# A down projection in two column chunks at once, with seven block products in place of eight for 14 of its 44 pair steps

## The chip, the cores and the metric

The kernel runs on one core of one Trainium2 chip. The metric is the device time of one execution in microseconds (us). The kernel before takes 1144.04 us, the median of three runs (1143.70 to 1145.09).

## The reference

One decoder layer on x of 256 tokens by 2048 features, in float32: a token mixer with three head groups and an output projection, and then a SwiGLU feed-forward part. The change touches only the last matrix product of it:

```python
mix = jnp.concatenate([y_ret, y_diff, y_sgu], axis=-1) @ w_out[l]
x = x + rms_norm(mix, post_mix_g[l])
h = rms_norm(x, pre_ffn_g[l])
f = (jax.nn.silu(h @ w_gate[l]) * (h @ w_up[l])) @ w_down[l]
x = x + rms_norm(f, post_ffn_g[l])
```

FFN_HIDDEN is 5632, so `w_down` is 5632 by 2048.

## The kernel before, in words

All large products run alike. Weights come from HBM in pieces of two K-blocks (2 x 128 rows) by 512 columns, 512 KB each. `split_weights` (L74 to L81) loads a piece on SP's queue into a tile `raw` (pool `wraw`, four buffers), ACT casts it to a rounded `hi` (L78), and DVE writes the remainder `lo` = raw - hi (L80). `hi` and `lo` come from the pool `wsplit`, five buffers each. The activations are split in the same way. `accumulate` (L83 to L89) then makes one 128x128 by 128x512 block product as three matmuls into one PSUM bank: hi by hi (L87), lo by hi (L88), hi by lo (L89). `matmul_chunk` does this for one chunk of 512 output columns: over the pieces, for both blocks of 128 tokens and both K-blocks of a piece, twelve matmuls per piece. With `lead=3` the second token block runs three pieces behind the first, so that the first one's result can be worked on early; that is used at the last chunk of `w_out`, at the first of `w_gate` and at the last of `w_down`.

After `w_out` the second normalisation (`second_norm`, L484 to L499) forms the input `x1_hi`, `x1_lo` of the feed-forward part, with transposes on TensorE (`x1_ps`, L495). Then come eleven chunks of `w_gate` and `w_up`, whose results, multiplied and transposed, are kept as `h` in five tiles. Before the down projection ACT copies two of these to other places (`near`, L597). The down projection is four `matmul_chunk` calls, one per 512 output columns, of 22 pieces each. Each chunk's result is multiplied by the gain `gp` into `fg` and squared for the row sums (L608, L609); for the last chunk ACT squares the bank directly (L620), DVE joins the partial sums (L621), GpSimd takes the power -0.5 (L623), and DVE scales, adds the residual (L627) and SP stores.

A Tile layer schedules the instructions: it sets each engine's order and puts a wait wherever a buffer of a pool is used again. Each engine then runs its own list in order.

Of the kernel before, what the change touches and what calls it, by code (L numbers as in the profile page):

```python
# [33 lines left out]
def trunk(  # L34
# [580 lines left out]
    nc.vector.tensor_reduce(out=part_ss, in_=ss_f[:, :, 0:3], axis=AX.X, op=ALU.add)  # L615
    nc.vector.tensor_scalar(out=part_ss, in0=part_ss, scalar1=1.0 / D, scalar2=EPS, op0=ALU.mult, op1=ALU.add)

    def last_down(tb, acc):
# [5 lines left out]
        nc.vector.tensor_tensor(out=fg[:, tb, cs], in0=acc, in1=gp[:, cs], op=ALU.mult)  # L624
        for c0, c1 in ((0, 512), (512, 1024), (1024, 1536), (1536, 2048)):
# [95 lines left out]
```

## Time and profile before

| | |
|---|---|
| median of 3 runs | 1144.04 us (1143.70 to 1145.09) |
| the profiled execution's own time | 1144.55 us |
| its span in the trace | 1142.8 us |
| busy in the span: PE, DVE, ACT | 1131.9 us, 636.5 us, 536.0 us |
| moved by DMA | 221.34 MB, mean 194 GB/s |

The span is the time from the first to the last instruction of the program; 1.75 us of the execution lie outside. PE is the matmul side of TensorE and PEld its weight loads, which overlap the matmuls; a matmul's busy time overlaps that of the next one, so that the distance between starts, not the busy time, tells what one costs.

### The profile page before, as it was taken

Reading aid. Unit: us, or ns where it says so; the run is one execution under the profiler, and the core shown is the slowest. Engines: PE = TensorE matmul, PEld = TensorE weight load, DVE = VectorE, ACT = ScalarE, POOL = GpSimd, SP = SyncE. Lnnn points to the kernel's source line nnn. Section 1 sums busy time; section 2 is a strip of 40 time slices with the busy share of each in tenths; the row PEclk is TensorE's granted clock in tenths of the full one; section 3 lists DMA queues with packets and bytes.
Section 4 is the critical chain, followed back from the end, with each engine's and each line's share of the span. In section 5 each row is a group of like instructions: output and inputs, shape, how many; then the busy total and the mean of one; then the engine's idle time right before and its main releaser. Section 6 shows DMA issues by size and latency. Waiting matters only on the chain.

```text
span 1142.8 us, 13922 instructions
## 1 busy us (share of the span) xinstructions
PE 1131.9 (99%) x5280; PEld 952.9 (83%) x5280; DVE 636.5 (56%) x759; ACT 536.0 (47%) x729; POOL 26.5 (2%) x55
## 2 busy tenths in 40 slices
...
PEclk9999999999999999999999999999999999999999
...
GB/s 352 267 189 186 164 158 181 166 223 185 180 220 225 166 150 227 192 188 187 188 192 189 187 191 193 186 197 188 186 192 191 199 213 197 189 198 190 165 199 111
DMA packets 64580, 221.34 MB, mean 194 GB/s; under 512 B 7296, under 2 KB 9344, under 8 KB 63872
## 3 DMA queue, kind: packets, MB, share of 16 engines
...
## 4 chain that ended last, share of the span: by engine, by line
PE 98%; issue 1%; DMA 0%; DVE 0%; ACT 0%; DVEq 0%; POOLq 0%; POOL 0%; ACTq 0%
PE acc L87 32%; PE acc L89 31%; PE acc L88 31%; PE h_ps L579 1%; PE qk_ps L235 0%; PE sc L267 0%; DMA xt<-in_xT_dram 0%; PE x_ps L495 0%; PE yt_ps L191 0%; PE o_ps L243 0%; PE o_ps L244 0%; PE o_ps L242 0%; PE sc L344 0%; DVE fg L627 0%; PE pm L421 0%
## 5 line engine op out<-in xcount | busy, mean ns | idle before, releaser
L80 DVE TENSOR_TENSOR lo<-raw,hi 128x1024 fp32r<-128x1024 f32 (+2 forms) x409 | 485.8, 1190 | 446.7 <-ACT hi L78 426.2
L78 ACT CAST hi<-raw 128x1024 fp32r<-128x1024 f32 (+2 forms) x409 | 416.6, 1021 | 532.6 <-PE acc L88 474.0
L87 PE MATMUL acc<-hi,x_hi 128*128 128x512 f32 (+1 forms) x1152 | 444.5, 386 | 1.1 <-DVE x_hi L181 1.1
L88 PE MATMUL acc<-hi,x_lo 128*128 128x512 f32 (+1 forms) x1152 | 438.7, 381 | 0.0
L89 PE MATMUL acc<-lo,x_hi 128*128 128x512 f32 (+1 forms) x1152 | 438.6, 381 | 0.0
L87 PEld LDWEIGHTS acc<-hi,x_hi 128*128 128x128 f32 x1152 | 216.8, 188 | 39.8 <-issue 3.4
L89 PEld LDWEIGHTS acc<-lo,x_hi 128*128 128x128 f32 x1152 | 216.6, 188 | 38.4 <-DVE lo L80 0.4
L88 PEld LDWEIGHTS acc<-hi,x_lo 128*128 128x128 f32 x1152 | 216.9, 188 | 36.7 <-DVE x_lo L184 0.2
L87 PE MATMUL acc<-hi,h 128*128 128x512 f32 x224 | 87.2, 389 | 0.0
L89 PE MATMUL acc<-lo,h 128*128 128x512 f32 x224 | 87.1, 389 | 0.0
L88 PE MATMUL acc<-hi,h 128*128 128x512 f32 x224 | 87.1, 389 | 0.0
L87 PE MATMUL acc<-hi,y_hi 128*128 128x512 f32 x128 | 50.3, 395 | 0.0
L88 PE MATMUL acc<-hi,y_lo 128*128 128x512 f32 x128 | 49.8, 391 | 0.0
L87 PE MATMUL acc<-hi,near 128*128 128x512 f32 x128 | 49.8, 389 | 0.0
L88 PE MATMUL acc<-hi,near 128*128 128x512 f32 x128 | 49.8, 389 | 0.0
L89 PE MATMUL acc<-lo,near 128*128 128x512 f32 x128 | 49.8, 389 | 0.0
L89 PE MATMUL acc<-lo,y_hi 128*128 128x512 f32 x128 | 49.8, 390 | 0.0
L89 PEld LDWEIGHTS acc<-lo,h 128*128 128x128 f32 x224 | 42.1, 188 | 8.8
L87 PEld LDWEIGHTS acc<-hi,h 128*128 128x128 f32 x224 | 42.1, 188 | 8.7
L88 PEld LDWEIGHTS acc<-hi,h 128*128 128x128 f32 x224 | 42.1, 188 | 8.6
L89 PEld LDWEIGHTS acc<-lo,near 128*128 128x128 f32 x128 | 24.0, 188 | 5.0
L87 PEld LDWEIGHTS acc<-hi,near 128*128 128x128 f32 x128 | 24.0, 188 | 5.0
...
## 6 DMA issues: line engine op xcount, KB each, us to landing
raw<-in_w_gate_dram SPq DMA_DIRECT2D x88, 512.0 KB, 3.5
raw<-in_w_up_dram SPq DMA_DIRECT2D x88, 512.0 KB, 3.5
raw<-in_w_down_dram SPq DMA_DIRECT2D x88, 512.0 KB, 4.3
raw<-in_w_ret_dram SPq DMA_DIRECT2D x47, 512.0 KB, 4.1
...
raw<-in_w_out_dram SPq DMA_DIRECT2D x32, 512.0 KB, 3.8
raw<-in_w_sgu_dram SPq DMA_DIRECT2D x16, 512.0 KB, 4.0
...
```

What stands on the lines that cost most here:

```text
L78: nc.scalar.copy(out=hi, in_=raw)
L80: nc.vector.tensor_tensor(out=lo, in0=raw, in1=hi.bitcast(F32), op=ALU.subtract)
L87: nc.tensor.matmul(ps, lhsT=a_hi, rhs=wh, start=first, stop=False)
L88: nc.tensor.matmul(ps, lhsT=a_lo, rhs=wh, start=False, stop=False)
L89: nc.tensor.matmul(ps, lhsT=a_hi, rhs=wl, start=False, stop=last)
L579: nc.tensor.transpose(out=pt[:, i], in_=aa[tb][:, i * P:(i + 1) * P], identity=ident)
```

## The change

The down projection works on two column chunks at once, first columns 0 to 1023, then 1024 to 2047, in `down_columns`. A step takes one pair p of K-blocks for both chunks: two pieces of weights, `ra` and `rb`. A pair step of kind P (`plain_pair`) is what stood there before: eight block products, 24 matmuls. A step of kind S (`seven_products`) sees tokens and weights as 2 x 2 blocks and makes seven products with sums of blocks, 21 matmuls. The sums of the activations are made once for the pairs 4 to 11 (`token_sums`, DVE and ACT) and kept where `x1_hi` and `x1_lo` were. The sums of the weights are made in each S step by DVE, in place in `ra` and `rb`, and then split by a second round of casts and remainders. The order of the steps is written out as a string: PPPSPPSPPSPPSPPSPPSP for the first half (6 S) and PPPPSPSPSPSPSPSPSPSP for the second (8 S); two more P pairs close each half, first for one token block and then for the other. The products that belong to single results go to banks 1, 2, 3 and 7, the shared ones to banks 0, 4, 5 and 6, and `partial_sums` adds these up after the last S. The copies `near` go. The pool `wsplit` has four buffers in place of five, in the whole kernel; `lead=3` stays at `w_out` and `w_gate`.

```diff
@@ -59,7 +59,7 @@
 
     const = ctx.enter_context(tc.tile_pool(name="const", bufs=1))
     act = ctx.enter_context(tc.tile_pool(name="act", bufs=1))
-    wsplit = ctx.enter_context(tc.tile_pool(name="wsplit", bufs=5))
+    wsplit = ctx.enter_context(tc.tile_pool(name="wsplit", bufs=4))
     wraw = ctx.enter_context(tc.tile_pool(name="wraw", bufs=4, side="right"))
...
-    for i, tag in ((2, "a_hi"), (3, "a_lo")):
-        near = act.tile([P, 2, 8, T], F32R, tag=tag, name=f"near{i}")
-        for j in range(2):
-            part, k0 = h_parts[2 * i + j]
-            for q in range(2):
-                nc.scalar.copy(out=near[:, q, k0:k0 + 4], in_=part[:, q, k0:k0 + 4])
-            h_parts[2 * i + j] = (near, k0)
-    gp = hfar.tile([P, D], F32, tag="h3", name="gp")
-    fg = hfar.tile([P, NT, D], F32, tag="h2", name="fg")
-    load_in_order(gp, post_ffn.partition_broadcast(P))
...
-    for n in range(3):
-        matmul_chunk(w_down[n], HB, 512, h_of, on_tb=lambda tb, acc, n=n: down_evac(n, tb, acc))
...
-    def last_down(tb, acc):
-        cs = slice(1536, 2048)
-        nc.scalar.activation(out=fg[:, tb, cs], in_=acc, func=AF.Square, accum_out=ss_f[:, tb, 3:4])
...
+    dn = ctx.enter_context(tc.tile_pool(name="dn", bufs=1))
...
+    def token_sums(i, c):
+        hi, lo = h_chunk(c)
+        tmp = dn.tile([P, 2, 1024], F32, tag="wide", name="sums_f")
+        a = tmp[:, 0].rearrange("p (q e t) -> p q e t", q=2, e=2)
+        f = tmp[:, 1].rearrange("p (q s t) -> p q s t", q=2, s=4)
+        nc.vector.tensor_tensor(out=tmp[:, 0].rearrange("p (k t) -> p k t", k=4), in0=hi.bitcast(F32),
+                                in1=lo.bitcast(F32), op=ALU.add)
+        a11, a21 = a[:, :, 0, TB[0]], a[:, :, 0, TB[1]]
+        a12, a22 = a[:, :, 1, TB[0]], a[:, :, 1, TB[1]]
+        nc.vector.scalar_tensor_tensor(out=f[:, :, 0], in0=a21, scalar=-1.0, in1=a22, op0=ALU.mult, op1=ALU.subtract)
+        nc.vector.scalar_tensor_tensor(out=f[:, :, 1], in0=f[:, :, 0], scalar=-1.0, in1=a11, op0=ALU.mult,
+                                       op1=ALU.subtract)
+        nc.vector.tensor_tensor(out=f[:, :, 2], in0=a11, in1=a21, op=ALU.subtract)
+        nc.vector.tensor_tensor(out=f[:, :, 3], in0=a12, in1=f[:, :, 1], op=ALU.subtract)
+        home = homes[i // 2]
+        flat = tmp[:, 1]
+        s_hi = home[:, 0, i % 2].rearrange("p q s t -> p (q s t)")
+        s_lo = home[:, 1, i % 2].rearrange("p q s t -> p (q s t)")
+        nc.scalar.copy(out=s_hi, in_=flat)
+        nc.vector.tensor_tensor(out=s_lo, in0=flat, in1=s_hi.bitcast(F32), op=ALU.subtract)
+        for q in range(2):
+            sums[2 * c + q] = [(home[:, 0, i % 2, q, j], home[:, 1, i % 2, q, j]) for j in range(4)]
...
+    def plain_pair(n0, p, tbs=(0, 1)):
+        out = []
+        for j, banks in ((0, (1, 3)), (1, (2, 7))):
+            hi, lo = split_weights(w_down[n0 + j][p], 2, 512)
+            out.append([(banks[tb], h_block(2 * p + e, tb), (hi[:, e], lo[:, e])) for e in range(2) for tb in tbs])
+        return out
+    def seven_products(n0, p):
+        ra, rb = fetch(n0, p), fetch(n0 + 1, p)
+        h1 = wsplit.tile([P, 2, 512], F32R, tag="hi", name="hi")
+        l1 = wsplit.tile([P, 2, 512], F32R, tag="lo", name="lo")
+        h22 = dn.tile([P, 512], F32R, tag="h22", name="hi_22")
+        l22 = dn.tile([P, 512], F32R, tag="l22", name="lo_22")
+        nc.scalar.copy(out=h1, in_=ra)
+        nc.scalar.copy(out=h22, in_=rb[:, 1])
+        lo_of(l1, ra, h1)
+        lo_of(l22, rb[:, 1], h22)
+        for out, in0, in1, op in ((ra[:, 0], ra[:, 0], rb[:, 0], ALU.subtract), (rb[:, 0], rb[:, 1], rb[:, 0], ALU.subtract),
+                                  (rb[:, 1], rb[:, 1], ra[:, 0], ALU.add), (ra[:, 1], ra[:, 1], rb[:, 1], ALU.subtract)):
+            nc.vector.tensor_tensor(out=out, in0=in0, in1=in1, op=op)
+        h2 = wsplit.tile([P, 2, 512], F32R, tag="hi", name="hi_sa")
+        l2 = wsplit.tile([P, 2, 512], F32R, tag="lo", name="lo_sa")
+        h3 = wsplit.tile([P, 2, 512], F32R, tag="hi", name="hi_sb")
+        l3 = wsplit.tile([P, 2, 512], F32R, tag="lo", name="lo_sb")
+        nc.scalar.copy(out=h2, in_=ra)
+        lo_of(l2, ra, h2)
+        nc.scalar.copy(out=h3, in_=rb)
+        lo_of(l3, rb, h3)
+        s1n, s2, s3, s4 = sums[p]
+        return [[(0, h_block(2 * p, 0), (h1[:, 0], l1[:, 0])),
+                 (1, h_block(2 * p + 1, 0), (h1[:, 1], l1[:, 1])),
+                 (2, s4, (h22, l22))],
+                [(4, s1n, (h2[:, 0], l2[:, 0])),
+                 (3, h_block(2 * p + 1, 1), (h2[:, 1], l2[:, 1]))],
+                [(6, s3, (h3[:, 0], l3[:, 0])),
+                 (5, s2, (h3[:, 1], l3[:, 1]))]]
...
+        def partial_sums():
+            u = dn.tile([P, 512], F32, tag="u", name="u")
+            nc.scalar.copy(out=fg[:, 0, 0:512], in_=banks[0])
+            nc.vector.tensor_tensor(out=u, in0=fg[:, 0, 0:512], in1=banks[5], op=ALU.add)
+            nc.vector.tensor_tensor(out=fg[:, 0, 512:1024], in0=u, in1=banks[4], op=ALU.add)
+            nc.vector.tensor_tensor(out=fg[:, 1, 512:1024], in0=fg[:, 0, 512:1024], in1=banks[6], op=ALU.add)
+            nc.vector.tensor_tensor(out=fg[:, 1, 0:512], in0=u, in1=banks[6], op=ALU.add)
+        for i, (k, p) in enumerate(seq):
+            if i in extra:
+                extra[i]()
+            for part in (plain_pair(n0, p) if k == "P" else seven_products(n0, p)):
+                for b, a, w in part:
+                    product(b, a, w)
+            advance()
+            if i == last_s:
+                fg = new_fg()
+                partial_sums()
+        parts = [plain_pair(n0, p) for p in tail_pairs]
+        where = {1: (0, 0), 2: (0, 1), 3: (1, 0), 7: (1, 1)}
+        for tb in range(NT):
+            for group in zip(*parts):
+                for prods in group:
+                    for b, a, w in prods:
+                        if where[b][0] == tb:
+                            product(b, a, w)
+            for b in ((1, 2), (3, 7))[tb]:
+                finish(n0, tb, where[b][1], fg, banks[b], gp)
...
+    def close_chunk(n0, tb, j, fg, bank, gp):
+        cs = slice(j * 512, (j + 1) * 512)
+        n = n0 + j
+        nc.vector.tensor_tensor(out=fg[:, tb, cs], in0=fg[:, tb, cs], in1=bank, op=ALU.add)
+        sq = dn.tile([P, 512], F32, tag="u", name="sq_f")
+        nc.scalar.activation(out=sq, in_=fg[:, tb, cs], func=AF.Square, accum_out=ss_f[:, tb, n:n + 1])
+        nc.vector.tensor_tensor(out=fg[:, tb, cs], in0=fg[:, tb, cs], in1=gp[j], op=ALU.mult)
...
+    down_columns(0, lambda: new_fg(dn, "wide"), sequence("PPPSPPSPPSPPSPPSPPSP", [4, 5, 6, 7, 8, 9], [0, 1, 2, 3, 10, 11] + list(range(12, 20))),
+                 {0: lambda: token_sums(0, 2), 4: lambda: token_sums(1, 3), 10: lambda: token_sums(2, 4),
+                  16: lambda: token_sums(3, 5)}, close_chunk, [20, 21])
...
+    def close_last(n0, tb, j, fg, bank, gp):
+        if j == 0:
+            close_chunk(n0, tb, j, fg, bank, gp)
+            nc.vector.tensor_reduce(out=part_ss[:, tb:tb + 1], in_=ss_f[:, tb, 0:3], axis=AX.X, op=ALU.add)
+            nc.vector.tensor_scalar(out=part_ss[:, tb:tb + 1], in0=part_ss[:, tb:tb + 1], scalar1=1.0 / D, scalar2=EPS,
+                                    op0=ALU.mult, op1=ALU.add)
+            return
+        cs = slice(512, 1024)
+        nc.vector.tensor_tensor(out=fg[:, tb, cs], in0=fg[:, tb, cs], in1=bank, op=ALU.add)
+        sq = dn.tile([P, 512], F32, tag="u", name="sq_f")
+        nc.scalar.activation(out=sq, in_=fg[:, tb, cs], func=AF.Square, accum_out=ss_f[:, tb, 3:4])
         nc.vector.scalar_tensor_tensor(out=ss_t[:, tb:tb + 1], in0=ss_f[:, tb, 3:4], scalar=1.0 / D,
                                        in1=part_ss[:, tb:tb + 1], op0=ALU.mult, op1=ALU.add)
         nc.gpsimd.tensor_tensor(out=ro_f[:, tb:tb + 1], in0=ss_t[:, tb:tb + 1], in1=neg_half[:, :1], op=ALU.pow)
-        nc.vector.tensor_tensor(out=fg[:, tb, cs], in0=acc, in1=gp[:, cs], op=ALU.mult)
-        for c0, c1 in ((0, 512), (512, 1024), (1024, 1536), (1536, 2048)):
-            cs = slice(c0, c1)
-            nc.vector.scalar_tensor_tensor(out=fg[:, tb, cs], in0=fg[:, tb, cs], scalar=ro_f[:, tb:tb + 1],
-                                           in1=x_sb[:, tb, cs], op0=ALU.mult, op1=ALU.add)
-            nc.sync.dma_start(out=out[tb * P:(tb + 1) * P, cs], in_=fg[:, tb, cs])
-
-    matmul_chunk(w_down[3], HB, 512, h_of, lead=LEAD, on_tb=last_down)
+        nc.vector.tensor_tensor(out=fg[:, tb, cs], in0=fg[:, tb, cs], in1=gp[1], op=ALU.mult)
...
+    down_columns(2, lambda: new_fg(hlow, "h0"), sequence("PPPPSPSPSPSPSPSPSPSP", [4, 5, 6, 7, 8, 9, 10, 11], plain[:12]), {}, close_last, [20, 21])
```

In the rows below, of the built programs' order, lines of the changed kernel have their own numbers: L632 is `lo_of`, L658 the four sums of weights, L628 the load of an S step, L702 to L704 are the three matmuls of a block product, L741 and L744 stand in `close_chunk`, L765 to L780 in `close_last`. A number behind a name is the buffer's.

**The pair steps, DVE.** Before, DVE's list in the down projection is remainders alone, one per piece, with the evacuation of a chunk now and then:

```order
L80 TENSOR_TENSOR lo_8184<-raw_8180,hi_8182 128x1024
L80 TENSOR_TENSOR lo_8202<-raw_8198,hi_8200 128x1024
L80 TENSOR_TENSOR lo_8220<-raw_8216,hi_8218 128x1024
L80 TENSOR_TENSOR lo_8238<-raw_8234,hi_8236 128x1024
L80 TENSOR_TENSOR lo_8256<-raw_8252,hi_8254 128x1024
```

Now, in the second half, from the second S step (buffers 8445 and 8447) over the P step behind it (8490 and 8496) to the start of the third S step:

```order
L632 TENSOR_TENSOR lo_8450<-raw_8445,hi_8449 128x1024
L632 TENSOR_TENSOR lo_22_8452<-raw_8447,hi_22_8451 128x512
L658 TENSOR_TENSOR raw_8445<-raw_8445,raw_8447 128x512
L658 TENSOR_TENSOR raw_8447<-raw_8447 128x512
L658 TENSOR_TENSOR raw_8447<-raw_8447,raw_8445 128x512
L658 TENSOR_TENSOR raw_8445<-raw_8445,raw_8447 128x512
L632 TENSOR_TENSOR lo_sa_8462<-raw_8445,hi_sa_8461 128x1024
L632 TENSOR_TENSOR lo_sb_8464<-raw_8447,hi_sb_8463 128x1024
L80 TENSOR_TENSOR lo_8494<-raw_8490,hi_8492 128x1024
L80 TENSOR_TENSOR lo_8500<-raw_8496,hi_8498 128x1024
L632 TENSOR_TENSOR lo_8531<-raw_8526,hi_8530 128x1024
```

An S step has eight DVE instructions in a row where two P-like remainders stood.

**The loads, SP.** The same stretch on SP's queue, with what each load waits for:

```order
L628 DMA raw_8445<-in_w_down_dram 128x1024 [waits DMAHW7_49,DVE_49]
L628 DMA raw_8447<-in_w_down_dram 128x1024 [waits DMAHW4_49,DMAHW0_49,DVE_49]
L76 DMA raw_8490<-in_w_down_dram 128x1024 [waits DMAHW1_49,DVE_49]
L76 DMA raw_8496<-in_w_down_dram 128x1024 [waits DMAHW6_49,DMAHW2_49,DVE_49]
L628 DMA raw_8526<-in_w_down_dram 128x1024 [waits DMAHW3_49,DVE_49]
L628 DMA raw_8528<-in_w_down_dram 128x1024 [waits DMAHW4_49,DVE_49]
```

An S and a P step take four loads, as many as `wraw` has buffers, so 8526 is the buffer of 8445 again: its wait for DVE is for `lo_sa_8462`, the last reader of that buffer, and that of 8528 is for `lo_sb_8464`.

**From `w_out` to `w_gate`, PE.** Before, the matmuls of the first `w_gate` chunk for the first token block up to the transposes for the second (`x1_ps_3761`):

```order
L89 MATMUL acc_3796<-lo_3802,x1_hi_3257 128x512
L87 MATMUL acc_3796<-hi_3812,x1_hi_3257 128x512
L88 MATMUL acc_3796<-hi_3812,x1_lo_3258 128x512
L89 MATMUL acc_3796<-lo_3814,x1_hi_3257 128x512
L87 MATMUL acc_3796<-hi_3812,x1_hi_3257 128x512
L88 MATMUL acc_3796<-hi_3812,x1_lo_3258 128x512
L89 MATMUL acc_3796<-lo_3814,x1_hi_3257 128x512
L495 MATMUL x1_ps_3761<-ident_100,hx_3245 128x128 x4
```

Now the same place:

```order
L89 MATMUL acc_3796<-lo_3802,x1_hi_3257 128x512
L87 MATMUL acc_3796<-hi_3812,x1_hi_3257 128x512
L88 MATMUL acc_3796<-hi_3812,x1_lo_3258 128x512
L495 MATMUL x1_ps_3761<-ident_100,hx_3245 128x128 x4
L495 MATMUL x1_ps_3769<-ident_100,hx_3245 128x128 x4
L87 MATMUL acc_3797<-hi_3800,x1_hi_3257 128x512
L495 MATMUL x1_ps_3777<-ident_100,hx_3245 128x128 x4
```

The products with `lo_3814` now stand behind the transposes of the second token block. On DVE, the list before around that block's normalisation:

```order
L498 TENSOR_TENSOR x1_lo_3258<-x1_ps_3777,x1_hi_3257 128x4x128
L510 TENSOR_TENSOR mg_3243<-acc_3570,gpm_3246 128x512
L80 TENSOR_TENSOR lo_3826<-raw_3822,hi_3824 128x1024
L498 TENSOR_TENSOR x1_lo_3258<-x1_ps_3785,x1_hi_3257 128x4x128
L80 TENSOR_TENSOR lo_3838<-raw_3834,hi_3836 128x1024
```

And now:

```order
L498 TENSOR_TENSOR x1_lo_3258<-x1_ps_3777,x1_hi_3257 128x4x128
L510 TENSOR_TENSOR mg_3243<-acc_3570,gpm_3246 128x512
L80 TENSOR_TENSOR lo_3814<-raw_3810,hi_3812 128x1024
L498 TENSOR_TENSOR x1_lo_3258<-x1_ps_3785,x1_hi_3257 128x4x128
L80 TENSOR_TENSOR lo_3826<-raw_3822,hi_3824 128x1024
```

Each remainder stands one piece later than it did: `lo_3814`, the second piece of `w_gate`'s first chunk, is where `lo_3826`, the third, was.

## Rows read from the trace of the kernel before

**Rows 1.** The page's head, parts 1 and 2: busy time by engine, granted clock

```profile
span 1142.8 us, 13922 instructions
PE 1131.9 (99%) x5280; PEld 952.9 (83%) x5280; DVE 636.5 (56%) x759; ACT 536.0 (47%) x729; POOL 26.5 (2%) x55
PEclk9999999999999999999999999999999999999999
```

**Rows 2.** The page's part 4, chain that ended last, shares by engine

```profile
PE 98%; issue 1%; DMA 0%; DVE 0%; ACT 0%; DVEq 0%; POOLq 0%; POOL 0%; ACTq 0%
```

**Rows 3.** Stretches: us, busy time by engine, PEclk, DMA share, GB/s

```profile
905.00:1080.00 175.00, 175.00 (x774) 144.96 (x773) 85.16 (x75) 71.65 (x78) 0.00 (x0) 1.00 0.63 204
```

**Rows 4.** Timeline, PE at the end: start us, us, engine, line, op

```profile
1129.11 0.39 PE L89 MATMUL acc<-lo,h 128*128 128x512 f32 x1
...
1131.83 0.39 PE L89 MATMUL acc<-lo,h 128*128 128x512 f32 x1
```

**Rows 5.** The page's part 5, one matmul of the down projection

```profile
L87 PE MATMUL acc<-hi,h 128*128 128x512 f32 x224 | 87.2, 389 | 0.0
```

**Rows 6.** Costs by line and shape, ACT: busy us, mean ns

```profile
L78 ACT CAST hi<-raw 128x1024 fp32r<-128x1024 f32 x359 | 375.5, 1049 | 487.7 <-PE acc L88 443.6 <-issue 22.4 <-DMA raw<-in_w_out_dram 6.7
L597 ACT CAST near<-h 128x1024 fp32r<-128x1024 f32 x8 | 7.7, 1045 | 1.7 <-PE acc L88 1.7
L78 ACT CAST hi<-raw 128x512 fp32r<-128x512 f32 x2 | 1.2, 610 | 0.0
```

**Rows 7.** Costs by line and shape, DVE

```profile
L80 DVE TENSOR_TENSOR lo<-raw,hi 128x1024 fp32r<-128x1024 f32 x359 | 438.5, 1224 | 404.7 <-ACT hi L78 388.0 <-PE h_ps L579 14.9 <-PE acc L88 0.3
L194 DVE SCALAR_TENSOR_TENSOR y_lo<-yt_ps,cols,y_hi 128x256 fp32r<-128x256 f32 x16 | 7.5, 478 | 0.0
L80 DVE TENSOR_TENSOR lo<-raw,hi 128x512 fp32r<-128x512 f32 x2 | 1.4, 688 | 0.0
L624 DVE TENSOR_TENSOR fg<-acc,gp 128x512 f32<-128x512 f32 x2 | 1.4, 684 | 0.0
```

**Rows 8.** The page's part 6, DMA issues: KB each, us to landing

```profile
raw<-in_w_gate_dram SPq DMA_DIRECT2D x88, 512.0 KB, 3.5
raw<-in_w_down_dram SPq DMA_DIRECT2D x88, 512.0 KB, 4.3
```

**Rows 9.** Timeline, DVE at the start of the down projection

```profile
904.13 4.63 DVE L80 TENSOR_TENSOR lo<-raw,hi 128x1024 fp32r<-128x1024 f32 x4
909.98 1.23 DVE L80 TENSOR_TENSOR lo<-raw,hi 128x1024 fp32r<-128x1024 f32 x1 [1.22 <-ACT hi L78]
920.95 1.23 DVE L80 TENSOR_TENSOR lo<-raw,hi 128x1024 fp32r<-128x1024 f32 x1 [1.49 <-ACT hi L78]
```

**Rows 10.** Timeline, ACT at the same place

```profile
908.89 1.05 ACT L78 CAST hi<-raw 128x1024 fp32r<-128x1024 f32 x1 [1.96 <-DMA raw<-in_w_down_dram]
911.44 1.05 ACT L78 CAST hi<-raw 128x1024 fp32r<-128x1024 f32 x1 [1.50 <-DMA raw<-in_w_down_dram]
919.87 1.05 ACT L78 CAST hi<-raw 128x1024 fp32r<-128x1024 f32 x1 [1.67 <-PE acc L88]
```

**Rows 11.** Timeline, PE, from w_out to w_gate

```profile
407.03 0.63 PE L495 MATMUL x_ps<-ident,hx 128*128 128x128 f32 x4
413.03 0.39 PE L89 MATMUL acc<-lo,x_hi 128*128 128x512 f32 x1
```

**Rows 12.** Timeline, DVE, the same stretch

```profile
411.58 1.22 DVE L80 TENSOR_TENSOR lo<-raw,hi 128x1024 fp32r<-128x1024 f32 x1
```

**Rows 13.** Timeline, end of the program

```profile
1134.97 0.60 ACT L620 ACTIVATE fg<-acc 128x512 f32<-128x512 f32 x1 [4.75 <-PE acc L89]
1135.70 0.16 DVE L621 SCALAR_TENSOR_TENSOR ss_t<-ss_f,part_ss 128x1 f32<-128x1 f32 x1 [1.88 <-ACT fg L620]
1135.93 0.55 POOL L623 TENSOR_TENSOR ro_f<-ss_t,neg_half 128x1 f32<-128x1 f32 x1 [4.89 <-DVE ss_t L621]
1136.52 2.74 DVE L627 SCALAR_TENSOR_TENSOR fg<-fg,ro_f,x_sb 128x512 f32<-128x512 f32 x4
```

More of the change, by code (lines that the diff above doesn't have):

```diff
@@ L615, in trunk @@
-    nc.vector.tensor_reduce(out=part_ss, in_=ss_f[:, :, 0:3], axis=AX.X, op=ALU.add)
-    nc.vector.tensor_scalar(out=part_ss, in0=part_ss, scalar1=1.0 / D, scalar2=EPS, op0=ALU.mult, op1=ALU.add)
-    def last_down(tb, acc):
-        cs = slice(1536, 2048)
-        nc.scalar.activation(out=fg[:, tb, cs], in_=acc, func=AF.Square, accum_out=ss_f[:, tb, 3:4])
+    part_ss = const.tile([P, NT], F32, tag="part_ss", name="part_ss")
+    TB = (slice(0, P), slice(P, 2 * P))
+    sums = {}
+    homes = [act.tile([P, 2, 2, 2, 4, P], F32R, tag=tag, name=f"sums_{tag}") for tag in ("a_hi", "a_lo")]
@@ new lines, in fetch, with lo_of, h_block @@
+    def fetch(n, p):
+        raw = wraw.tile([P, 2, 512], F32, tag="raw", name="raw")
+        nc.sync.dma_start(out=raw, in_=w_down[n][p])
+        return raw
+    def lo_of(lo, raw, hi):
+        nc.vector.tensor_tensor(out=lo, in0=raw, in1=hi.bitcast(F32), op=ALU.subtract)
+    def h_block(kb, tb):
+        hi, lo = h_of(kb)
+        return hi[:, TB[tb]], lo[:, TB[tb]]
+    def plain_pair(n0, p, tbs=(0, 1)):
[4 more added lines that the diff above has]
+        return out
@@ new lines, in bank_tile, with down_columns, product @@
+    def bank_tile(i):
+        pool, tag = ((ps_tr, "tr"), (ps_acc, "acc"), (ps_acc, "acc"), (ps_acc, "acc"), (ps_tr, "tr"), (ps_mx, "mx"),
+                     (ps_mx, "mx"), (ps_acc, "acc"))[i]
+        return pool.tile([P, 512], F32, tag=tag, name=f"bank{i}")
+    def down_columns(n0, new_fg, seq, extra, finish, tail_pairs):
+        gp = [ft.tile([P, 512], F32, tag="fa", name="gp") for _ in range(2)]
+        for j in range(2):
+            load_in_order(gp[j], post_ffn[(n0 + j) * 512:(n0 + j + 1) * 512].partition_broadcast(P))
+        banks = {}
+        kinds = [k for k, _ in seq]
+        last_s = max(i for i, k in enumerate(kinds) if k == "S")
+        left = {}
+        for i, (k, _) in enumerate(seq):
+            for b, n in (((1, 2), (2, 2), (3, 2), (7, 2)) if k == "P" else tuple((b, 1) for b in range(7))):
+                left[b] = left.get(b, 0) + n
+        for b, n in ((1, 2), (2, 2), (3, 2), (7, 2)):
+            left[b] += n * len(tail_pairs)
+        begun = set()
+        def product(b, a, w):
+            if b not in banks:
+                banks[b] = bank_tile(b)
+            left[b] -= 1
+            (a_hi, a_lo), (w_hi, w_lo) = a, w
+            nc.tensor.matmul(banks[b], lhsT=a_hi, rhs=w_hi, start=b not in begun, stop=False)
+            nc.tensor.matmul(banks[b], lhsT=a_lo, rhs=w_hi, start=False, stop=False)
+            nc.tensor.matmul(banks[b], lhsT=a_hi, rhs=w_lo, start=False, stop=left[b] == 0)
+            begun.add(b)
+        part = {}
+        def partial_sums():
[25 more added lines that the diff above has]
+                finish(n0, tb, where[b][1], fg, banks[b], gp)
```

18 lines of the change are left out of this document (13 added, 5 removed).

## The prediction, made before the changed kernel ran

> **What bounds the kernel now.** I read the page's busy shares first, then the chain, then the stretch that is changed. PE is busy 1131.9 of 1142.8 us and the granted clock is full in every slice [rows 1], which of the two levels is 2.4 GHz. The chain that ended last is 98% PE [rows 2]. In the down projection PE has no gap in 175 us, while DVE works 85.16 us and ACT 71.65 [rows 3]: the weights are split well ahead, and PE alone sets the time. What does one matmul cost there? Its busy time is 389 ns [rows 5], but neighbours overlap: twelve starts lie in 1131.83 - 1129.11 = 2.72 us [rows 4], so one costs **0.2267 us** of the stream. That is the price of a matmul taken away, as long as PE stays the bound. DVE and ACT, half idle, are the engines to watch, since the change trades PE's work for theirs.
>
> The sum is made against the profiled execution, 1144.55 us, half a microsecond over the median of the runs shown, 1144.04. About 0.2%, some 2.3 us, is what a measurement here can tell from no change.
>
> **A, matmuls taken out.** 14 S steps, each with seven products for eight, three matmuls a product: 42 x 0.2267 = **-9.5**. (By the busy time it would be 42 x 0.389 = -16.3, but the starts decide.) The eight copies `near`, 1.045 each on ACT [rows 6], count nothing: PE's stream runs past them.
>
> **B, the second half, S and P in turn.** A pair of steps gives PE 21 + 24 = 45 matmuls, 10.2 us. What does it ask of the others? On DVE a P step has two remainders of 1.224; an S step has `lo`, `lo_sa` and `lo_sb` of the same size, `lo_22` of 0.688 and four sums, which no row shows; the nearest is an addition of 128x512 in float32 at 0.684 to 0.688 [rows 7], and I take 0.69. So 2.45 + 3 x 1.22 + 5 x 0.69 = 9.6, below 10.2: DVE by its sum of work holds. But the work forms a ring with the loads. S and P together use all four `wraw` buffers, and an S step keeps both of its until `lo_sa` and `lo_sb` are done; only then do the next S step's two loads start. Nothing of that step can be done before they land. The ring, from the end of `lo_sb`:
>
> - the load of `rb` until its cast can start: a `w_down` piece takes 4.3 from issue to landing against 3.5 in `w_gate` [rows 8]. At the start of the down projection loads follow one another as closely as here: four remainders run from 904.13, starting 1.13 apart (4.63 less one of 1.23, by 3), so that the first two end at 905.36 and 906.49, and the casts of those refilled buffers start at 908.89 and 911.44 [rows 9, 10], 3.53 and 4.95 later. `rb` is such a second load; I take 4.5, nearer to it than to the median, with 3.45 and 5.3 (4.95 and as much again as it lies over my value, less a little) as ends
> - cast `hi_22` 0.61 [rows 6], `lo_22` 0.69, four sums 2.76, cast `hi_sa` 1.05, `lo_sa` 1.22, `lo_sb` 1.13 (joined remainders start so far apart, [rows 9]), and some 0.15 for hand-overs between engines: 7.6
>
> That is **12.1** a period against PE's 10.2: PE waits 1.9 in each of the seven periods behind the first S, 13.3. The ring starts with a lead of 3.5, since at the first S, when buffers come free, PE has 53 matmuls ahead (12.0) before it needs `lo_sb`, and DVE and ACT need some 8.5. So **+9.8**. With 3.45 for the load the period is 11.1 and B +2.8; with 5.3 it is 12.9 and B +15.4.
>
> Here a page of the Trainium skill differs from the rows. "DMA: Bandwidth & Descriptors", section "Anatomy of one DMA — SWDGE (gpsimd) path", gives a fixed 2.0 us plus the bytes at 436 GB/s, an estimate of 3.2 us for 512 KB; by it the period would be 10.8, B about +0.7 and the whole sum about -0.7. The page's fit is for another path than SP's, and this case's pieces of that size land in 3.5 to 4.3 [rows 8], so the measurement decides.
>
> **C, the first half.** S, P and P give PE 69 matmuls, 15.6. A ring over the loads runs there too, but with a P step between: the load behind `lo_sb` is that of the second P, and from it follow cast 1.05, its remainder, `lo`, `lo_22`, four sums, cast, `lo_sa`, `lo_sb`: with 4.5 for the load 14.8, so it just holds. The token sums are the disturbance. DVE's list from the last `w_up` evacuation to the second S step's `lo_sb` holds three of the four: 13 remainders of 1.22, 15.9; two of 0.69 and eight sums of 0.69, 6.9; four evacuations of some 0.7, 2.8; per token sum two of 1.22 and four of 128x256, which no row shows in this form and for which I take 0.478 [rows 7], 4.35 x 3 = 13.1. In all 38.7. PE has till then 158 matmuls and two groups of transposes, 36.6. The lack is 2.1, and waits for ACT in between add to it: **+3.0** (ends 0, if the list starts early, and 6).
>
> **D, `wsplit` with four buffers.** With `lead=3` four pieces are alive, so none is prefetched. Where `w_out` meets `w_gate`, PE fills the time of the second token block's normalisation with products of the first. It now has twelve fewer of them ahead of the transposes at 407.03 [rows 11], 2.72 of work, because the piece that those twelve need is split only where the next one was: at 411.58 to 412.80 on DVE [rows 12], just ahead of PE's use at 413.03 [rows 11], so DVE has no earlier place to give; 0.6 more for the transposes themselves, which nothing covers: **+3.3** (0, if the refill is quick, to 5). Elsewhere a plain chunk keeps one piece in use and three ahead: nothing.
>
> **E, between the halves** all eight banks and four split buffers are in use: **+0.3** (0 to 1).
>
> **F, the end.** Now ACT's square of 0.60 reads the bank at once, then L621, the power, L627 [rows 13]. In the changed kernel DVE adds the partial sums first (0.69), and the first chunk's gain product, row sum and gain product of the second stand on DVE between square and power: some 0.8. **+1.5** (0.7 to 2).
>
> Sum: -9.5 + 9.8 + 3.0 + 3.3 + 0.3 + 1.5 = **+8.4**: 1152.95 for the profiled execution, 1152.4 beside the median.
>
> **The rivals.**
>
> *Faster: the loads keep up.* If the second S load lands in 3.45 and less (few other loads are in flight while DVE works on the sums), and C and D stay at their low ends, the sum is -9.5 + 2.8 + 0.3 + 0.7 = -5.7, about 1138; with C or D in part, up to 1141. For it: pieces in `w_gate` do land in 3.5 [rows 8]. Against: the two refills above took 3.53 and 4.95 [rows 9, 10], and with either the ring exceeds PE's turn. The point that decides is a load to cast of 2.6: there the period equals 10.2. Chance 0.17.
>
> *No change.* B at a landing of 3.9 (+6), the rest half of what I put: 1142 to 1146. Chance 0.17.
>
> *Slower still.* Landings of 5.3 in a burst and C and D at their upper ends: -9.5 + 15.4 + 5 + 4.5 + 2 = +17, 1161. Part of the slower case, chance 0.15 of the 0.66.
>
> *The clock.* PE has waits of 2 us in turn, and no row before shows what the granted clock does behind such a wait. If it went to the lower level for part of the second half, each matmul at twice the price, 100 of them would cost 23 us: over 1170. Chance 0.03.
>
> That the change doesn't do what it says is no rival: the program has 42 block matmuls fewer.
>
> **How the numbers follow.** My forecast holds 0.48 (1147 to 1158), slower still with the clock 0.18, the other two 0.17 each: faster 0.17, within the bound 0.17, slower 0.66. The range 1141 to 1161 takes in the load from about 3.6 to 5.3 with the other terms at either end and leaves out the best loads and the clock.
>
> **What the profile after would show.** PE's idle time is in the second half, in gaps of about 2 us that repeat every 12 us and end with `lo_sa` or `lo_sb`; SP's S loads wait for DVE, and ACT's casts of them wait for the load. The first half has one or two gaps early, of 1 to 3 us; near 404 to 410 one gap of some 3; the power in the tail about 1.5 later behind the last matmul. Additions of 128x512 take 0.69, and the granted clock stays at full. I am wrong in B if PE runs through the second half without a repeated gap, in D if the stretch near 407 is as long as before, and in A if matmul starts lie apart by anything but 0.2267 where PE isn't waiting.

## The result, and the profile after

The changed kernel takes **1159.87 us**, the median of four runs (1158.53 to 1161.01), against 1144.57 (1143.70 to 1145.70) for the kernel before on the same chip, the three runs above and a fourth: 1.0130 times as long, 95% interval 1.0117 to 1.0142. That is 15.3 us slower; the forecast was 8.4 slower, its range up to 1161. The profiled execution took 1159.04, its span is 1157.3, 14.5 over the span before.

The page of the changed kernel (head, parts 1 and 2, the chain of part 4, two groups of part 5, the loads of part 6) answers to [rows 1, 2, 8]:

```profile
span 1157.3 us, 14036 instructions
PE 1129.9 (98%) x5238; PEld 943.8 (82%) x5238; DVE 720.2 (62%) x885; ACT 554.1 (48%) x755; POOL 25.4 (2%) x55
PEclk9999999999999999999999999999999999999998
...
PE 83%; DVE 7%; DMA 5%; ACT 2%; issue 2%; POOL 0%; ACTq 0%; DVEq 0%; POOLq 0%; SPq 0%
...
L663 ACT CAST hi_sa<-raw 128x1024 fp32r<-128x1024 f32 x14 | 14.7, 1047 | 52.4 <-DVE raw L658 52.4
L658 DVE TENSOR_TENSOR raw<-raw 128x512 f32<-128x512 f32 x56 | 38.6, 689 | 1.3
...
raw<-in_w_down_dram SPq DMA_DIRECT2D x88, 512.0 KB, 4.5
```

PE has 42 matmuls fewer, and yet the span is longer. In the chain PE has fallen from 98% to 83%; DVE, DMA and ACT stand in it with 14% together. An addition of weights takes 0.689, as assumed. Where does PE wait? Its timeline shows seven long waits (each line has the start and the duration, and in brackets at the end the idle time before it and what ended that):

```profile
409.06 1.29 PE L495 MATMUL x_ps<-ident,hx 128*128 128x128 f32 x8 [1.67 <-DVE hx L491]
...
1010.55 0.50 PE L704 MATMUL bank<-lo,h 128*128 128x512 f32 x1 [2.25 <-DVE lo L80]
...
1078.08 0.50 PE L702 MATMUL bank<-hi_sa,sums_a_hi 128*128 128x512 f32 x1 [1.38 <-ACT hi_sa L663]
1090.10 0.50 PE L702 MATMUL bank<-hi_sa,sums_a_lo 128*128 128x512 f32 x1 [1.36 <-ACT hi_sa L663]
1102.06 0.50 PE L702 MATMUL bank<-hi_sa,sums_a_lo 128*128 128x512 f32 x1 [1.41 <-ACT hi_sa L663]
1114.34 0.50 PE L702 MATMUL bank<-hi_sa,sums_a_lo 128*128 128x512 f32 x1 [1.75 <-ACT hi_sa L663]
1126.29 0.50 PE L702 MATMUL bank<-hi_sa,sums_a_lo 128*128 128x512 f32 x1 [1.43 <-ACT hi_sa L663]
```

Five stand in the second half, 12.05 apart on average ((1126.29 - 1078.08) / 4). Behind the other two the granted clock stood at its lower level (1.2 GHz, half of full) for about 3 us, as the stretches show (us, busy time of PE, PEld, DVE, ACT, POOL, then the clock, DMA share, GB/s):

```profile
1025.00:1140.00 115.00, 106.55 (x461) 85.02 (x460) 87.46 (x95) 53.31 (x58) 0.00 (x0) 1.00 0.51 178
410.00:413.50 3.50, 3.49 (x13) 2.52 (x11) 2.89 (x6) 1.48 (x3) 0.00 (x0) 0.54 0.00 0
1011.30:1014.50 3.20, 3.20 (x9) 2.55 (x8) 1.71 (x3) 0.72 (x2) 0.00 (x0) 0.51 0.82 241
```

Told by places, from the starts of matching matmuls in both traces: up to the last `w_up` product +5.5, from there to the last matmul +6.2, behind it +2.7; together 14.5.

**The ring.** One period of the second half, DVE, ACT and SP's queue:

```profile
1079.20 1.22 DVE L632 TENSOR_TENSOR lo_sb<-raw,hi_sb 128x1024 fp32r<-128x1024 f32 x1
1079.31 1.46 SPq L628 DMA_DIRECT2D raw<-in_w_down_dram  x2
...
1082.93 1.05 ACT L652 CAST hi<-raw 128x1024 fp32r<-128x1024 f32 x1 [2.06 <-DMA raw<-in_w_down_dram]
1084.02 1.22 DVE L632 TENSOR_TENSOR lo<-raw,hi 128x1024 fp32r<-128x1024 f32 x1 [1.32 <-PE bank L704]
1084.77 0.62 ACT L653 CAST hi<-raw 128x512 fp32r<-128x512 f32 x1 [0.78 <-DMA raw<-in_w_down_dram]
1085.42 0.69 DVE L632 TENSOR_TENSOR lo<-raw,hi 128x512 fp32r<-128x512 f32 x1 [0.18 <-ACT hi L653]
1086.03 2.87 DVE L658 TENSOR_TENSOR raw<-raw 128x512 f32<-128x512 f32 x4
1089.01 1.04 ACT L663 CAST hi_sa<-raw 128x1024 fp32r<-128x1024 f32 x1 [3.62 <-DVE raw L658]
...
1090.08 1.22 DVE L632 TENSOR_TENSOR lo_sa<-raw,hi_sa 128x1024 fp32r<-128x1024 f32 x1 [1.19 <-ACT hi_sa L663]
...
1091.22 1.22 DVE L632 TENSOR_TENSOR lo_sb<-raw,hi_sb 128x1024 fp32r<-128x1024 f32 x1
```

From the start of one `lo_sb` to that of the next 12.02 us pass, of which 4.35 from its end (1080.42) to the cast of `rb`'s block (1084.77). PE's own share of a period is 10.2.

### The profile page after: what moved, and what is told of

It reads as the page before. It is cut to its first block, busy times and chain, and to the rows that moved or that the text cites. A ratio compares the mean times of both kernels' runs of the same rounds, so it can differ in the third digit from the quotient of the medians.

```text
span 1157.3 us, 14036 instructions
## 1 busy us (share of the span) xinstructions
PE 1129.9 (98%) x5238; PEld 943.8 (82%) x5238; DVE 720.2 (62%) x885; ACT 554.1 (48%) x755; POOL 25.4 (2%) x55
## 4 chain that ended last, share of the span: by engine, by line
PE 83%; DVE 7%; DMA 5%; ACT 2%; issue 2%; POOL 0%; ACTq 0%; DVEq 0%; POOLq 0%; SPq 0%
PE acc L87 24%; PE acc L89 24%; PE acc L88 23%; DMA raw<-in_w_down_dram 4%; PE bank L704 3%; PE bank L703 3%; PE bank L702 3%; DVE raw L658 2%; DVE lo L80 1%; ACT hi_sa L663 1%; DVE lo_sb L632 1%; PE h_ps L579 1%; DMA gpm<-in_post_mix_dram 1%; DVE lo L632 1%; DMA xt<-in_xT_dram 0%
## 5 line engine op out<-in xcount | busy, mean ns | idle before, releaser
L80 DVE TENSOR_TENSOR lo<-raw,hi 128x1024 fp32r<-128x1024 f32 (+2 forms) x381 | 450.1, 1187 | 350.3 <-ACT hi L78 327.6
L78 ACT CAST hi<-raw 128x1024 fp32r<-128x1024 f32 (+2 forms) x381 | 386.4, 1018 | 436.0 <-PE acc L88 374.2
L704 PE MATMUL bank<-lo,h 128*128 128x512 f32 x268 | 104.3, 392 | 2.2 <-DVE lo L80 2.2
L702 PE MATMUL bank<-hi,h 128*128 128x512 f32 x268 | 105.3, 393 | 0.6 <-ACT hi L78 0.6
L703 PE MATMUL bank<-hi,h 128*128 128x512 f32 x268 | 105.0, 392 | 0.0
L704 PEld LDWEIGHTS bank<-lo,h 128*128 128x128 f32 x268 | 50.7, 189 | 13.6 <-DVE lo L80 3.0
L702 PEld LDWEIGHTS bank<-hi,h 128*128 128x128 f32 x268 | 50.7, 189 | 11.8 <-ACT hi L78 1.3
L703 PEld LDWEIGHTS bank<-hi,h 128*128 128x128 f32 x268 | 50.6, 189 | 10.5
L658 DVE TENSOR_TENSOR raw<-raw 128x512 f32<-128x512 f32 x56 | 38.6, 689 | 1.3
L632 DVE TENSOR_TENSOR lo<-raw,hi 128x512 fp32r<-128x512 f32 (+1 forms) x28 | 26.3, 957 | 13.3 <-ACT hi L652 10.7
L89 PEld LDWEIGHTS acc<-lo,y_hi 128*128 128x128 f32 x128 | 24.0, 188 | 6.6 <-DVE lo L80 1.6
L87 PEld LDWEIGHTS acc<-hi,y_hi 128*128 128x128 f32 x128 | 24.0, 188 | 5.4 <-ACT hi L78 0.5
```

Source lines behind the costliest of these rows:

```text
L78: nc.scalar.copy(out=hi, in_=raw)
L80: nc.vector.tensor_tensor(out=lo, in0=raw, in1=hi.bitcast(F32), op=ALU.subtract)
L87: nc.tensor.matmul(ps, lhsT=a_hi, rhs=wh, start=first, stop=False)
L89: nc.tensor.matmul(ps, lhsT=a_hi, rhs=wl, start=False, stop=last)
L632: nc.vector.tensor_tensor(out=lo, in0=raw, in1=hi.bitcast(F32), op=ALU.subtract)
L658: nc.vector.tensor_tensor(out=out, in0=in0, in1=in1, op=op)
```

## The experiments

The factor of each run is against runs of the kernel before on the same chip; those had medians of 1144.57 beside the changed kernel, 1144.96 beside the first four runs below, 1145.53 beside the run without partial sums and the very last one, and 1144.79 beside the other four. Where a text says so many us "less than the change", it is a plain difference from 1159.87; by the factors such a difference is up to 1 us smaller or larger.

**Four split buffers alone**, in the kernel before:

```diff
-    wsplit = ctx.enter_context(tc.tile_pool(name="wsplit", bufs=5))
+    wsplit = ctx.enter_context(tc.tile_pool(name="wsplit", bufs=4))
```

> The kernel before with one edit: four split buffers in place of five. In the profile of the changed kernel the last w_up product of the feed-forward part stands 5.5 us later than before (1.9 of it at w_out, 3.6 at the transposes behind it). If four split buffers alone cause this (theory), this kernel takes 1144.5 + 5.5 = 1150 (1149 to 1151.5), with a wait of PE of 1.7 near 407 and a stretch at the lower clock behind it. If the down projection's own tiles or order cause it (rival), it stays at 1144 to 1145.5.

Measured 1153.53, 1.0078 of before (1.0063 to 1.0093), more than expected. The last `w_up` product is late by 5.4, as in the changed kernel, with the same wait:

```profile
409.65 1.29 PE L495 MATMUL x_ps<-ident,hx 128*128 128x128 f32 x8 [1.68 <-DVE hx L491]
...
410.90:414.40 3.50, 3.26 (x17) 2.13 (x16) 3.42 (x6) 2.22 (x5) 0.00 (x0) 1.00 0.00 0
```

So the buffer causes the first 5.5 us. One part of the expectation failed: behind this wait the clock stayed at 1.00 (second row, read as the stretches above). Another 3.2 are lost in the old down projection: 1.1 at its start and 2.1 in its last chunk, which also runs with `lead=3`.

**A fifth split buffer again, up to the first `w_up` chunk**, in the changed kernel (the pool closes with the mixer's pools):

```diff
+        count[0] += 1
+        wsplit = extra[0] if extra and count[0] % 5 == 0 else wsplit4
...
+        extra.append(mctx.enter_context(tc.tile_pool(name="wsplit_x", bufs=1)))
```

> The changed kernel with a fifth split buffer up to the end of the first w_gate and w_up chunk (every fifth piece is split in a pool of one buffer that closes there), and four from then on. If the 5.5 us come from the lead of three over four live pieces at w_out and w_gate (theory), this takes 1159.9 - 5.5 = 1154.4 (1153.5 to 1155.5) and the last w_up product stands where it stood before. If the missing buffer costs its time in the later chunks or in the down projection (rival), it stays over 1158.

Measured 1154.62, 1.0090 (1.0073 to 1.0107): 5.3 less than the change, and the last `w_up` product stands 0.4 from where it stood before (the first product of `w_out` already does). The theory holds.

**A fifth raw buffer**, in the changed kernel:

```diff
-    wraw = ctx.enter_context(tc.tile_pool(name="wraw", bufs=4, side="right"))
+    wraw = ctx.enter_context(tc.tile_pool(name="wraw", bufs=5, side="right"))
...
-            u = dn.tile([P, 512], F32, tag="u", name="u")
+            u = fg[:, 1, 0:512]
...
-        sq = dn.tile([P, 512], F32, tag="u", name="sq_f")
-        nc.scalar.activation(out=sq, in_=fg ...
+        nc.scalar.activation(out=bank, in_=fg ...
```

> The changed kernel with five buffers for raw weights in place of four; for the room the square's unused result goes into the bank and the first partial sum into its final place, which adds no instruction. Ring theory: an S step's first load no longer waits for the S step before, its second only for lo_sa. The ring shortens from 12.0 by lo_sb's 1.14 and by the load's time beside a second one, 0.7, to 10.2, about PE's own 10.2: the waits in the second half (0.65, 1.54, 1.52, 1.57, 1.91, 1.59) nearly go, -7 (-5 to -9), 1151 to 1155. Rival, DVE's work of 9.6 per 10.2 with its hand-overs is what runs out: the waits stay above 1 us each and the time within 2 of 1159.9.

Measured **1142.01**, 0.9979 (0.9970 to 0.9988): 17.9 less than the change, and faster than the kernel before. The waits of the second half are gone, and so is the one between the halves:

```profile
1000.00:1128.00 128.00, 128.00 (x566) 105.56 (x565) 104.70 (x120) 63.44 (x75) 0.93 (x1) 1.00 0.54 189
```

PE runs 128 us without a gap beside a DVE busy 104.7. So DVE's work was not the bound; the rival falls. The gain was more than twice what was expected and lies outside the expected range: in the profiles, the second half gives 10.8 (its waits, 8.8 and 0.8, and shorter distances between starts), the place between the halves some 4 and the part up to the down projection 1.5.

**The first half's order in the second half too:**

```diff
-    ... sequence("PPPPSPSPSPSPSPSPSPSP", [4, 5, 6, 7, 8, 9, 10, 11], plain[:12]), ...
+    ... sequence("PPPSPPSPPSPPSPPSPPSP", [4, 5, 6, 7, 8, 9], [0, 1, 2, 3, 10, 11] + list(range(12, 20))), ...
```

> The changed kernel with the first half's order of steps in the second half too: six S steps with two P between, in place of eight with one. Six matmuls more, +1.4. Ring theory: with two P between, the load behind lo_sb is a P step's and the chain of 14.8 lies under PE's 15.6, so the waits of 8.8 us go: 1159.9 + 1.4 - 8.8 = 1152.5 (1151 to 1154). Rival, S steps cost PE a wait of 1.5 each whatever stands between: two waits fewer, about -3 + 1.4, 1158.

Measured 1151.16, 1.0059 (1.0044 to 1.0074), with four raw buffers and six matmuls more: within the range of the ring theory, but not for its reason alone. In the profile the repeated waits of the second half are gone; two of some length are left, 0.70 and 1.26 beyond the usual distance of starts. With the added matmuls the second half gained 6.4, not 7.4. Nearly 3 came between the halves, which this edit leaves as they were: there the wait was 1.15 in place of 2.25, and the clock stayed up.

**`rb`'s sums cast and split first:**

```diff
+        nc.scalar.copy(out=h3, in_=rb)
+        lo_of(l3, rb, h3)
         nc.scalar.copy(out=h2, in_=ra)
         lo_of(l2, ra, h2)
-        nc.scalar.copy(out=h3, in_=rb)
-        lo_of(l3, rb, h3)
```

> The changed kernel with the cast and the remainder of rb's sums ahead of those of ra's in an S step. Ring theory: rb's sums are done one addition earlier, so the cast runs beside the last addition, and the ring is shorter by that addition and the hand-over, 0.7 us, in each of the six periods with a wait: 1159.9 - 4 = 1156 (1155 to 1157.5). Rival, the loads alone set the rhythm (two loads' landing, whatever order releases them) or DVE's sum of work does: no change, 1159 to 1161.

Measured 1153.09, 1.0077 (1.0060 to 1.0094), 6.8 less. The period, from cast to cast:

```profile
1083.84 1.05 ACT L663 CAST hi_sb<-raw 128x1024 fp32r<-128x1024 f32 x1 [2.87 <-DVE raw L658]
...
1095.10 1.05 ACT L663 CAST hi_sb<-raw 128x1024 fp32r<-128x1024 f32 x1 [2.87 <-DVE raw L658]
```

is 11.26, 0.76 shorter; 0.7 was expected. A link of the ring taken out shortens the period by itself, and the second half gained 4.2 in the profile. The rest, 3.6, came between the halves, where the wait fell from 2.25 to 0.42 and the clock stayed up; how much of that is the edit's is not shown, since the place differs between executions (under E below).

**P steps alone**, with five raw buffers:

```diff
-    down_columns(0, ..., sequence("PPPSPPSPPSPPSPPSPPSP", ...), {0: lambda: token_sums(0, 2), ...}, close_chunk, [20, 21])
+    down_columns(0, ..., [("P", p) for p in range(20)], {}, close_chunk, [20, 21])
...
-        nc.vector.tensor_tensor(out=fg[:, tb, cs], in0=fg[:, tb, cs], in1=bank, op=ALU.add)
+        nc.vector.tensor_copy(out=fg[:, tb, cs], in_=bank)
```

> The changed kernel with five raw buffers and P steps alone: no S step, no sums of tokens or weights, no partial sums (the bank is copied where it was added); 42 matmuls more. Theory A: a matmul is worth the distance of starts, 42 x 0.2267 = 9.5, PE being the bound with and without: 1142.0 + 9.5 = 1151.5 (1150.5 to 1152). Rival one, a matmul is worth its busy time: + 16.3, 1158. Rival two, the five raw buffers gained in other places and the S steps save little: 1143 to 1147.

Measured 1151.30, 1.0061 (1.0046 to 1.0076): 9.3 more than with S steps and the same buffers. Once the loads keep up, the 42 matmuls are worth the distance of their starts.

**No partial sums**, in the changed kernel:

```diff
-                partial_sums()
+                nc.gpsimd.memset(fg, 0.0)
```

> The changed kernel without the partial sums: their place is set to zero by GpSimd, and the products gathered in the four shared banks are left out of the result; all matmuls stay. Between the halves PE waited 2.42 near 1010 and then ran at the lower clock for some 1.4 us more. If DVE's three partial sums, 1.9 us ahead of the remainder that PE waited for, are the cause (theory 1), that wait falls below 0.7 and the slow stretch with it: -3 (-2 to -4.5), 1157 (1155.4 to 1158). If the loads of the last four pieces, which start late and land in 5.9 to 7.2 us, are the cause by themselves (theory 2), the wait stays over 1.5 and the time within 1 of 1159.9.

In the changed kernel, three of the four additions stood among the last remainders like this:

```profile
1006.46 1.05 ACT L78 CAST hi<-raw 128x1024 fp32r<-128x1024 f32 x1 [0.28 <-DMA raw<-in_w_down_dram]
1007.36 0.68 DVE L713 TENSOR_TENSOR fg<-u,bank 128x512 f32<-128x512 f32 x1
1008.07 0.69 DVE L714 TENSOR_TENSOR fg<-fg,bank 128x512 f32<-128x512 f32 x1
...
1008.67 0.68 DVE L715 TENSOR_TENSOR fg<-u,bank 128x512 f32<-128x512 f32 x1
1009.27 2.35 DVE L80 TENSOR_TENSOR lo<-raw,hi 128x1024 fp32r<-128x1024 f32 x2
```

Measured 1158.98, 1.0114 (1.0098 to 1.0131), only 0.9 less. At its place theory 1 has it: beyond the usual distance of starts the wait fell from 2.42 to 0.62, and the slow stretch is gone.

```profile
1009.72 0.50 PE L704 MATMUL bank<-lo,h 128*128 128x512 f32 x1 [0.46 <-DVE lo L80]
```

But with all the sums in place two other profiles have 1.31 and 1.57 there and no slow stretch (under E below), so the sums are worth 0.7 to 1.8 of wait, and the slow stretch is not shown to be their doing. And the ring took the gain back in this run's profile: one load of `rb` landed late, 6.24 behind its issue against 4.4 to 4.6 in the periods around it,

```profile
1097.45 0.62 ACT L653 CAST hi<-raw 128x512 fp32r<-128x512 f32 x1 [2.80 <-DMA raw<-in_w_down_dram]
```

PE waited 3.6 for it, and the clock fell to the lower level behind that wait. One profile can't tell whether the other three runs lost it so, and how much the additions cost on average stays open. With five raw buffers all additions are there and PE has no wait, so loads that are issued late are needed for the wait too.

**The end.** With five raw buffers, the last products are sorted by their bank, so that PE runs the last twelve matmuls on bank 7 alone:

```diff
+            order = [t for group in zip(*parts) for prods in group for t in prods if where[t[0]][0] == tb]
+            if tb == 1:
+                order.sort(key=lambda t: where[t[0]][1])
...
```

> The changed kernel with five raw buffers, and in the closing of each half PE runs all products of the first chunk before those of the second for the second token block. Theory on the end: the first chunk's addition, square, gain product and row sum, which now stand between the last matmul and the power, run beside the last twelve matmuls: from 1142.0 to 1140.4 (1139.8 to 1141.3). Rival, the chain add, square, power, scale of the second chunk alone sets the end: 1141.6 to 1142.4.

Measured 1142.64, 0.9978 (0.9969 to 0.9988): no gain, but this tests nothing. `zip(*parts)` had given the first chunk's products of both pairs ahead of the second's all along, so the sort changes no order: in its trace PE, DVE, ACT and GpSimd have the same lists of instructions as with five raw buffers alone. The run is a repetition of that one, 0.6 apart from it, and neither the theory nor the rival was put to the test. What its trace shows holds for both: bank 3 is complete twelve matmuls, 2.7, before the end, but DVE has the first block's scaling in front, and the bank's addition starts at 1129.13, with the last matmul all but ended (1129.20):

```profile
1126.47 2.74 DVE L778 SCALAR_TENSOR_TENSOR fg<-fg,ro_f,x_sb 128x512 f32<-128x512 f32 x4 [0.44 <-POOL ro_f L773]
...
1129.13 0.68 DVE L741 TENSOR_TENSOR fg<-fg,bank 128x512 f32<-128x512 f32 x1
```

**The two buffers together** (the expectation counts the sort as a third edit), the fifth raw buffer in a pool that opens where the fifth split buffer's closes:

```diff
+        return extra_raw[0] if extra_raw and count[1] % 5 == 0 else wraw
...
+    extra_raw.append(ctx.enter_context(tc.tile_pool(name="wraw_x", bufs=1)))
```

> All three together: a fifth split buffer up to the end of the first w_gate and w_up chunk, a fifth raw buffer from there on (in a pool of its own), and the closing order of raw5_tail. If the three add up: 1142.0 - 4.0 (what raw5 still lost up to the down projection) - 1.5 = 1136.5 (1135.5 to 1138). If raw5's gain of 1.5 up to the down projection came from the fifth raw buffer there and both meet at w_gate, or the fifth raw buffer in its own pool fills late: 1138 to 1141.

Measured **1138.34**, 0.9947 (0.9932 to 0.9962), the best version. The two buffers add up (1142.0 - 4.0 = 1138.0, and the last `w_up` product stands 0.4 from where it stood before); the 1.5 for the end, which the sort could not give, is missing. To move the first block's scaling back,

```diff
+        if tb == 0:
+            late.append(scale_and_store)
+        else:
+            scale_and_store()
```

> As raw5_split5_tail, and the scaling and storing of the first token block is given to the scheduler behind the addition of the second block's first bank. In raw5_tail that addition could have started 2.7 us ahead of the last matmul, but DVE was scaling the first block until 1129.13, after the last matmul's start at 1128.8. If DVE's list is what holds the end (theory): 0.5 to 1 less than raw5_split5_tail, 1137.5 (1137 to 1138). If not: 1138 to 1139.

Measured 1138.54, 0.9940 (0.9925 to 0.9955): no gain. The addition of the first bank did move ahead, but the schedule left the first chunk's gain product and row sums and a scaling of the first block between the last matmul (1126.60) and the second bank's addition (1127.86). What the end can give back stays open.

## Why the prediction was right, and where it was not

The direction, the range and the main mechanism were right; the size was half, and that the time lies in the range is partly luck. 1159.87 is above the forecast's own band (1147 to 1158), in that of "slower still" (0.15), whose reason, landings of 5.3 and C and D at their upper ends, did not come: the landing was as forecast and C cost next to nothing. (That rival's sum also takes 5 and 4.5 for ends given as 6 and 5.) Of the signs named, PE's repeated waits came, but they end with the cast `hi_sa`, a link ahead of `lo_sa`, and the clock did not stay at full. By its own terms:

- **A, -9.5: right.** P steps alone cost 9.3 more.
- **B, +9.8: right.** The period is 12.0 (12.1 predicted), PE waits in six of the seven periods behind the first S, 0.65, then 1.54, 1.52, 1.57, 1.91 and 1.59 beyond the usual distance of starts, 8.8 in all. The load took 4.35 to the cast where I took 4.5, the rest 7.7 where I took 7.6. (The estimate of 3.2 worked out from the Trainium skill, "DMA: Bandwidth & Descriptors", section "Anatomy of one DMA — SWDGE (gpsimd) path", which the page gives for another path, is too low for SP's queue here: the first load of this period landed in 3.52 us, the second in 4.29.) Three runs show the cause from three sides: a buffer more, a link less, a step more between.
- **C, +3.0: failed, 0.3.** The list came out as counted, but I priced DVE's instructions by their busy time, though the prediction itself had 1.13 for joined remainders. DVE's rows (start, busy):

```profile
903.50 1.23 DVE L608 TENSOR_TENSOR sums_f<-h 128x1024 f32<-128x1024 f32 x1
904.64 1.22 DVE L80 TENSOR_TENSOR lo<-raw,hi 128x1024 fp32r<-128x1024 f32 x1
905.78 0.42 DVE L612 SCALAR_TENSOR_TENSOR sums_f<-sums_f 128x256 f32<-128x256 f32 x1
906.12 0.42 DVE L615 TENSOR_TENSOR sums_f<-sums_f 128x256 f32<-128x256 f32 x1
...
935.58 1.22 DVE L632 TENSOR_TENSOR lo_sb<-raw,hi_sb 128x1024 fp32r<-128x1024 f32 x1
```

  Starts lie 1.14 and 0.34 apart, not 1.22 and 0.478. From the `w_up` evacuation (899.53) to the second `lo_sb`'s end (936.80) 37.3 passed, not 38.7 and waits, and PE lost 0.3.
- **D, +3.3: undersized, 5.5.** "Elsewhere nothing" failed: `w_out` lost 1.8 up to the first transpose. The place that I priced lost 3.7, from the first transpose (400.82) to the second chunk of `w_gate` (455.75), 54.9 against 51.3 before. I had not thought of the clock, 0.54 of full in the 3.5 us behind the wait of 1.67, but it is the smaller part. Six other profiles have the same wait, 1.65 to 1.68, and the clock at 1.00 behind it: four split buffers alone, no partial sums, `rb` first, five raw buffers, their repetition, and P steps alone. They take 54.2 for the same stretch. This profile and the one with the first half's order twice, where the clock fell too, take 54.9 and 54.7. So four buffers cost 2.9 at this place and the clock 0.5 to 0.7 more; part of what it cost came back, since the next wait is 0.34 here and 1.05 to 1.06 in those six.
- **E, +0.3: failed, some 4 in this profile.** I looked at banks and buffers and not at the order on DVE: three partial sums stood ahead of the remainder that PE needed, and the loads of the last pieces were issued late and landed 5.9 to 7.2 later. To the wait of 2.4 the lower clock added seven distances 0.2 longer, 1.4. But the place differs from one execution to the next: the run with the first half's order twice and the one with a fifth split buffer up to `w_up` have the same lists on PE, DVE and ACT there, waited

```profile
1010.04 0.50 PE L704 MATMUL bank<-lo,h 128*128 128x512 f32 x1 [1.15 <-DVE lo L80]
...
1005.84 0.50 PE L712 MATMUL bank<-lo,h 128*128 128x512 f32 x1 [1.41 <-DVE lo L85]
```

  with the clock at 1.00 behind it, and lost 1.4 and 1.7 beyond the usual distances in place of 4.3. So E costs 1.4 to 4.3 by these three profiles.
- **F, +1.5: undersized, 2.7.** From the last matmul's end (1146.71) to the first scaling behind it 4.0 pass, 1.6 before [rows 13]; 0.3 are lost behind that. DVE's rows, ACT's second square and the power:

```profile
1144.14 2.74 DVE L780 SCALAR_TENSOR_TENSOR fg<-fg,ro_f,x_sb 128x512 f32<-128x512 f32 x4 [0.44 <-POOL ro_f L775]
1146.80 0.68 DVE L741 TENSOR_TENSOR fg<-fg,bank 128x512 f32<-128x512 f32 x1
1147.40 0.68 DVE L770 TENSOR_TENSOR fg<-fg,bank 128x512 f32<-128x512 f32 x1
...
1148.33 0.63 ACT L772 ACTIVATE sq_f<-fg 128x512 f32<-128x512 f32 x1
...
1149.87 0.16 DVE L773 SCALAR_TENSOR_TENSOR ss_t<-ss_f,part_ss 128x1 f32<-128x1 f32 x1
1150.11 0.55 POOL L775 TENSOR_TENSOR ro_f<-ss_t,neg_half 128x1 f32<-128x1 f32 x1 [6.00 <-DVE ss_t L773]
1150.69 2.74 DVE L780 SCALAR_TENSOR_TENSOR fg<-fg,ro_f,x_sb 128x512 f32<-128x512 f32 x4 [0.66 <-POOL ro_f L775]
```

  The first chunk's bank is complete 2.7 earlier, at 1143.99, but its addition stands on DVE behind the four scalings of the first token block, which end at 1146.88. So both additions and both squares come behind the last matmul. I counted one addition, the gain products and a row sum; the first chunk's addition and square, held back by that scaling, I did not.

The measured terms are -9.5, +8.8, +0.3, +5.5, +4, +2.7 and 0.8 at the second half's last pairs, in all +12.6 of 14.5; the other 1.9 are distances that are longer by less than 0.15 each. The step that failed most is E, by 3.7 in this profile, then C, by 2.7 the other way, and D, by 2.2. The clock, which I gave 0.03 as a rival of the second half, fell elsewhere, behind two waits, and cost some 2 us of the 14.5 (1.4 between the halves, 0.5 to 0.7 at the transposes).
